# Sums of weights loaded one at a time, and the last unit's second half added on VectorE

## The chip, the cores and the metric

The kernel runs on one core of a Trainium2 chip. The metric is the device time of one execution in microseconds; lower is better. Engines are named as in the profile: PE (TensorE, matrix products), PEld (its weight loads), DVE (VectorE), ACT (ScalarE), POOL (GpSimd), and SP (SyncE, which here only issues transfers). The core has 16 DMA engines, which all queues share.

## The reference, cut to what matters

One decoder block over 512 tokens plus 16 meta tokens, width 1024. After a LayerNorm the input is projected by `w_in` (1024 x 10240) to the queries, keys, values and gates of two attention branches of 8 and 16 heads, and to two merge gates:

```python
proj = jnp.einsum('bld,dn->bln', h, w_in[i])
q_d, k_d, v_d, g_d, q_s, k_s, v_s, g_s, m_d, m_s = jnp.split(proj, IN_OFFSETS, axis=-1)
...
outs_d.append(diff_attn_block(q_d[:, :, :, t0:t1], k_d[:, :, :, :t1], v_d[:, :, :t1], q_pos, slopes, lam))
outs_s.append(stick_breaking_block(q_s[:, :, t0:t1], k_s[:, :, :t1], v_s[:, :, :t1], q_pos))
...
br_d = jnp.einsum('blw,wd->bld', y_d * jax.nn.silu(g_d), w_br_diff[i])
br_s = jnp.einsum('blw,wd->bld', y_s * jax.nn.silu(g_s), w_br_sb[i])
merged = jax.nn.sigmoid(m_d + b_gate[i, 0]) * br_d + jax.nn.sigmoid(m_s + b_gate[i, 1]) * br_s
y = jnp.einsum('bld,de->ble', merged, w_out[i])
h = layer_norm(DN_ALPHA * h + y, ln_g[i], ln_b[i])
```

All of it is float32 at the interface.

## The kernel before, in words

**Products.** A float32 factor is split into a rounded high part and the rest, and a product is three matmuls: high by high, high by low, low by high. For weights, `prep` makes the split of one tile of 128 x 512: ACT writes `wh` (L183), DVE subtracts to get `wl` (L188). `wh` and `wl` have six buffers each, and `prep` is called four tiles ahead of the product that reads the tile.

**Units.** The work between the projections is 16 units in a row: eight `d` units (a differential head each, softmax) and eight `s` units (two stick-breaking heads each). During unit u the kernel also projects the keys and values of unit u+1 and the queries of unit u+2. Keys are computed position by position into `ks` and then stored by SP into the two key tiles `k` (L646, L647), eight small transfers per unit; the scores of the next unit (L759) read them, and a store can only start once the scores of the unit before have read the old keys.

**Sums of weights.** From the sixth unit on (`SEVEN = 5`), keys and values together are made with seven products of half-size blocks in place of eight. Three of the seven weight operands of a unit are sums of blocks of `w_in`: they are held in tiles `rawk` (five buffers). SP loads the first term (L144) and POOL's own DMA queue adds the others with an accumulating transfer (L146), four of these for each of the 11 units. `fetch` issues the loads whose buffers are free, sums first, and puts each accumulate on a list `later`, due 3 or 6 calls of `prep` later; `prep` calls `fetch` once. The pool of the `rawk` tiles is opened in unit `u + 4 == SEVEN`, that is u = 1. A helper, `placed`, holds each accumulate behind the POOL instruction that the program names before it; the first stage (up to `keep_order`) is held in program order too. Transfers on SP are not held so: the tile framework's scheduler places them by what they depend on. POOL runs its instructions in order; a POOL instruction that waits holds all behind it.

**POOL's other work in this stretch.** The bias of each `d` unit (L827, two buffers, so that it waits for the unit two before), the copy of meta columns (L663), and in each `s` unit two accumulating transfers `ys` (L935): the two heads of a unit leave PSUM in the wrong halves of the partitions, so ACT copies one half to `half` (L933), crossing partitions, and the other to `y` (L934), and POOL's transfer adds `half` to `y`.

**The last unit (p = 7).** Its `y` is the tile `ysT` itself. After it, DVE multiplies the gate in (L528), and DVE and ACT prepare the operands of the branch products (`operands`, L1038 to L1045), in tiles `gh`, `gl`, `t` that reuse the memory of the attention's tiles, `half` among them.

**Sync.** Each transfer on SP or ACT takes the next of eight semaphores in turn, so that the transfer eight places on waits until this one has landed.

Of the kernel before, what the change touches and what calls it, by code (L numbers as in the profile page):

```python
# [13 lines left out]
ALU = mybir.AluOpType  # L14
# [23 lines left out]
SEVEN = 5  # L38
# [7 lines left out]
def hybrid_block_kernel(ctx: ExitStack, tc: tile.TileContext, x, meta, emb_g, emb_b, w_in, b_gate,  # L46
                        diff_lambda, subln_g, w_br_d, w_br_s, w_out, ln_g, ln_b, out):
    nc = tc.nc
    v, s, g, pe = nc.vector, nc.scalar, nc.gpsimd, nc.tensor
# [76 lines left out]
    sum_loads, other_loads = [[l for l, x in enumerate(loads) if (x[2] == "rawk") == y] for y in (True, False)]  # L126
# [6 lines left out]

    def fetch(most=99):

        for order in (sum_loads, other_loads):
            while order and most:
                l = order[0]
                src, more, tag = loads[l]
                bufs, log = rings[tag]  # L140
                if len(log) >= bufs and left[log[-bufs]] or tag not in pools:
                    break
                raw = pools[tag].tile([P, 4, P], F32, tag=tag, name=tag, bufs=bufs)
                nc.sync.dma_start(raw if l < WOUT else raw.rearrange("p a b -> p (a b)"), src)  # L144
                if more is not None:
                    second[l] = [lambda raw=raw, x=x: g.dma_start(raw, x, accum_op=ALU.add) for x in more]  # L146
                    if tag == "rawa":
                        added(l)
                    else:
                        for n in range(len(more)):  # L150
                            later.append((state["n"] + 3 + 3 * n, lambda l=l: added(l)))
                        later.sort(key=lambda x: x[0])
                raws[l] = raw
                log.append(order.pop(0))
                most -= 1

    def added(l):

        if second.get(l):
            placed(second[l].pop(0), ORDERED[3:])  # L160
# [61 lines left out]
    def placed(work, engines=ORDERED):  # L222

        ins = nc.cur_bb.bb.instructions
        n = len(ins)
        work()
        for e in engines:
            new = next((i for i in ins[n:] if i.engine == e), None)
            old = next((ins[m] for m in range(n - 1, max(n - 400, 0), -1) if ins[m].engine == e), None)
            if new is not None and old is not None:  # L230
                follow(new, old)
# [153 lines left out]
    def query(n, o, w, k):  # L385

        pe.matmul(pss[n][:, ds(o, w)], raw0[:, n, k, :], hF[k][:, ds(M + o, w)], start=(k == 0), stop=(k == KT - 1))  # L387
# [3 lines left out]
    def high(half, k, copy):  # L391

        copy(hTh[:, k, HALF[half]], hF[k][:, HALF[half]])
# [55 lines left out]
    def lam2():  # L449
# [3 lines left out]
                 y=lambda h, k: query(1, 256 * h, 256, k), s=lambda h, k: high(h, k, s.copy),  # L453
# [129 lines left out]
    with tc.tile_pool(name="att", bufs=1) as ap:  # L583
# [334 lines left out]
        def s_values(unit, c, p, ta):  # L918
            V = unit["V"]
            v4, a4 = tails[c]  # L920
            own, oth = ((LO, HI), (HI, LO))[c]
            av = pav.tile([P, 512], F32, tag="av", name="av")
            pe.matmul(av, V[c][:, 0, :], ta[0][0], start=True, stop=False)
            pe.matmul(av[:, QOFF[4]:], v4, a4, start=False, stop=False)
            for j in range(1, 4):
                o = av[:, QOFF[j]:]
                pe.matmul(o, V[c][:, j, :], ta[j][0], start=False, stop=False)  # L927
                pe.matmul(o, V[c][:, j, :], ta[j][1], start=False, stop=False)
            pe.matmul(av, V[c][:, 0, :], ta[0][1], start=False, stop=True)
            if "y" not in unit:  # L930
                unit["y"] = gpool.tile([P, S], F32, tag="sg", name="ys")
            half = ap.tile([P, S], F32, tag="sq", name="half")
            s.copy(half[own], av[oth])  # L933
            s.copy(unit["y"][own], av[own])  # L934
            placed(lambda: g.dma_start(unit["y"][own], half[own], accum_op=ALU.add), ORDERED[3:])  # L935

        def keys_values(unit, kind, n):
            if UNITS.index((kind, n)) >= SEVEN:
                return [stage_kv(unit, kind, n)]
            return [stage_k(unit, kind, n), stage_v(unit, kind, n)]  # L940

        def spread(gen, t0, dt, count):
            return [(t0 + dt * m, lambda: next(gen)) for m in range(count)]
# [11 lines left out]
        pending = []  # L955
        for u, (kind, n) in enumerate(UNITS):
            unit = units[u]
            if u + 4 == SEVEN:
                pools["rawk"] = ap
            last = u + 1 == len(UNITS)  # L960
            proj = [] if last else keys_values(units[u + 1], *UNITS[u + 1])
            if u + 2 < len(UNITS):
                proj.append(stage_q(units[u + 2], *UNITS[u + 2]))
            steps = pending + [(0.6, lambda unit=unit: values(unit, kind))]
            pending = []
            if u + 1 < SEVEN:
                steps.append((9.2, store_k))
            if u in range(SEVEN - 5, SEVEN - 1):
                if not tS:
                    tS.append(ypool.tile([P, KT, L], F32R, tag="ys", name="tS"))  # L970
                steps.append((8.0, lambda k=u + 5 - SEVEN: placed(lambda: input_sums(k))))
            if u in GATE_AT and u < 14:
                proj.append(raw_gate(GATE_AT[u], kept["r"][GATE_AT[u]]))
            if kind == "d":
                ta = {}
                dt, t0, t1 = TD[u in GATE_AT]
                steps += spread(d_scores(unit, n), 0.0, dt, 10)
                parts = transposed(ta, apads[n % 2], "d")
                steps += [(t0 + 0.7 * m, f) for m, f in enumerate(parts)]
                steps.append((t1, lambda: d_values(unit, ta)))  # L980
                pending = [(3.0 if n < 7 else 5.8, lambda unit=unit, n=n: d_norm(unit, n))]
            else:
                if n == 0:
                    diag.append(ap.tile([P, L], F32, tag="bias", name="diag", bufs=2))
                    g.memset(diag[0], 0.0)
                    g.tensor_copy(diag[0][:, L - P:], ident)
                    for a in apads:
                        for i in range(NB):
                            g.memset(a[:, ds(AOFF[i] + NKEY[i] - 1, 1)], 0.0)
                if last:  # L990
                    ydT = [pair_of("ydT", n=S) for k in range(4)]
                    ydT = [ydT[k % 4][:, k // 4, :] for k in range(8)]
                    ysT = ypool.tile([P, 8, S], F32, tag="ys", name="ysT")
                    ysT = [ysT[:, k, :] for k in range(8)]
                    unit["y"] = ysT[7]

                    def fill_in(y, of):
                        placed(lambda: nc.sync.dma_start(y, of), [mybir.EngineType.SP])

                    fill_in(ydT[7], kept["d"][7])  # L1000
                    for m, (y, of) in enumerate(((ydT, "gd"), (ysT, "gs"))):
                        for j in range(7):
                            steps.append((1.3 + 1.5 * (7 * m + j), lambda o=y[j], x=kept[of][j]: fill_in(o, x)))
                    proj += [gate("d", n, lambda: ydT[7]), merge_gate(0, 0), merge_gate(0, 1), merge_gate(0, 2),
                             gate("s", n, lambda: ysT[7])]
                else:
                    if GATE_AT.get(u) == n:
                        yd = gpool.tile([P, S], F32, tag="sg", name="yd")
                        nc.sync.dma_start(yd, kept["d"][n])
                        proj.append(gate("d", n, lambda yd=yd: yd, kept["gd"][n]))  # L1010
                    else:
                        steps += zip((12.0, 24.0), late_gate(ap, *(kept[x][n] for x in ("d", "r", "gd"))))
                    proj.append(gate("s", n, lambda unit=unit: unit["y"], kept["gs"][n]))
                for c in range(2):
                    ta = {}
                    steps += spread(s_scores(unit, c, n == 0), (2.0 + 4.3 * c) if n == 0 else 4.4 * c, 0.85, 5)
                    parts = transposed(ta, apads[c], c)
                    steps += [(7.0 + 6.5 * c + 0.7 * m, f) for m, f in enumerate(parts)]
                    steps.append((10.5 + 6.5 * c, lambda c=c, ta=ta: s_values(unit, c, n, ta)))
            run(proj, steps)  # L1020
# [235 lines left out]
```

## Time and profile before

| | |
|---|---|
| time, median of 3 runs | 729.81 us (729.35 to 733.26) |
| the profiled execution's own time | 724.71 us |
| its span (first to last instruction) | 722.9 us |
| PE busy | 706.7 us (98%) |
| DVE busy | 571.3 us (79%) |
| ACT busy | 434.1 us (60%) |
| POOL busy | 127.6 us (18%) |
| mean granted PE clock | 0.996 |

A line of the profile reads "engine line operation out<-in"; a time in brackets is how long the engine sat idle before the instruction, and the name behind the arrow is what ended that. Busy time of matmuls counts their pipelined ends, so the idle time in brackets is a little shorter than the delay from start to start.

### The profile page before, as it was taken

Reading aid. Unit: us, or ns where it says so; the run is one execution under the profiler, and the core shown is the slowest. Engines: PE = TensorE matmul, PEld = TensorE weight load, DVE = VectorE, ACT = ScalarE, POOL = GpSimd, SP = SyncE. Lnnn points to the kernel's source line nnn. Section 1 sums busy time; section 2 is a strip of 40 time slices with the busy share of each in tenths; the row PEclk is TensorE's granted clock in tenths of the full one; section 3 lists DMA queues with packets and bytes.
Section 4 is the critical chain, followed back from the end, with each engine's and each line's share of the span. In section 5 each row is a group of like instructions: output and inputs, shape, how many; then the busy total and the mean of one; then the engine's idle time right before and its main releaser. Section 6 shows DMA issues by size and latency. Waiting matters only on the chain.

```text
span 722.9 us, 13508 instructions
## 1 busy us (share of the span) xinstructions
PE 706.7 (98%) x4558; PEld 644.5 (89%) x4558; DVE 571.3 (79%) x1253; ACT 434.1 (60%) x1043; POOL 127.6 (18%) x153
## 2 busy tenths in 40 slices
PE   9998999999999999999999999999999999999994
PEld 8998999989999888989989899988878998999884
DVE  6886897887796767979887898976267888788887
ACT  5674776767576677867767586765356456555300
POOL 3251110122122120212132110000003202130002
PEclk9999999999999999999999999999999999999998
DMA  9398544778989795798897956556539837787902
GB/s 293 95 171 180 158 101 122 171 159 194 217 170 201 196 183 153 163 234 165 219 208 177 227 137 188 146 154 190 167 90 197 173 108 186 142 167 195 325 18 102
DMA packets 182343, 123.64 MB, mean 171 GB/s; under 512 B 9041, under 2 KB 165106, under 8 KB 182274
## 3 DMA queue, kind: packets, MB, share of 16 engines
q1 hardware_dynamic: 148130, 102.32, 49.0%
q0 software_dynamic: 33824, 19.40, 21.6%
q10 hardware_dynamic: 320, 1.06, 0.4%
q8 instruction: 36, 0.59, 0.3%
q14 instruction: 33, 0.27, 0.1%
HBM read 91.96 MB, written 9.44 MB: 140 GB/s over the span
## 4 chain that ended last, share of the span: by engine, by line
PE 79%; DMA 6%; DVE 6%; ACT 4%; issue 3%; POOL 1%; SPq 0%; ACTq 0%; DVEq 0%; POOLq 0%
PE q L693 15%; PE ps L496 10%; PE ps L497 10%; PE ps L498 10%; PE q L1063 8%; PE ps L512 7%; PE sc L759 5%; PE t L765 3%; DMA k<-ks 2%; PE t L770 1%; DMA lgb<-in_ln_b_dram 1%; DMA ss<-sm 1%; PE bank L387 1%; PE av L927 1%; ACT wh L183 1%
## 5 line engine op out<-in xcount | busy, mean ns | idle before, releaser
L188 DVE TENSOR_TENSOR wl<-raw,wh 128x512 fp32r<-128x512 f32 x169 | 114.8, 686 | 45.8 <-ACT wh L183 40.9
L496 PE MATMUL ps<-hTh,wh 128*128 128x512 f32 x368 | 144.6, 393 | 1.5 <-ACT wh L183 1.5
L497 PE MATMUL ps<-hTl,wh 128*128 128x512 f32 x368 | 144.7, 393 | 0.0
L498 PE MATMUL ps<-hTh,wl 128*128 128x512 f32 x368 | 144.6, 393 | 0.0
L183 ACT CAST wh<-raw 128x512 fp32r<-128x512 f32 x169 | 103.0, 620 | 35.3 <-PE ps L497 26.4
L496 PEld LDWEIGHTS ps<-hTh,wh 128*128 128x128 f32 x368 | 69.2, 188 | 15.2 <-ACT wh L183 1.9
L146 POOL DMA_DIRECT2D rawk<-in_w_in_dram x44 | 58.7, 1649 | 131.2 <-DMA rawk<-in_w_in_dram 49.5
L498 PEld LDWEIGHTS ps<-hTh,wl 128*128 128x128 f32 x368 | 69.1, 188 | 14.0 <-DVE wl L188 0.4
L497 PEld LDWEIGHTS ps<-hTl,wh 128*128 128x128 f32 x368 | 69.2, 188 | 13.1
L759 PE MATMUL sc<-k,A 128*128 128x264 f32 (+3 forms) x320 | 67.9, 300 | 3.3 <-DMA k<-ks 3.1
L1063 PE MATMUL q<-gh,wh 128*128 128x256 f32 x224 | 63.5, 283 | 0.3 <-ACT t L1072 0.3
L1063 PE MATMUL q<-gl,wh 128*128 128x256 f32 x224 | 63.4, 283 | 0.0
L1063 PE MATMUL q<-gh,wl 128*128 128x256 f32 x224 | 63.4, 283 | 0.0
L776 DVE TENSOR_TENSOR al<-t,ah 128x512 fp32r<-128x512 f32 (+2 forms) x88 | 45.6, 525 | 22.2 <-ACT ah L775 18.4
L913 DVE TENSOR_TENSOR_SCAN e<-e,diag 128x528 f32<-128x528 f32 (+1 forms) x64 | 53.8, 846 | 7.0 <-ACT e L907 7.0
L775 ACT CAST ah<-t 128x288 fp32r<-128x288 f32 (+3 forms) x88 | 39.9, 462 | 29.9 <-PE t L765 20.0
L759 PEld LDWEIGHTS sc<-k,A 128*128 128x128 f32 x320 | 50.5, 189 | 6.5 <-issue 3.4
L693 PE MATMUL q<-tS,wh 128*128 128x264 f32 x176 | 50.8, 290 | 0.0
L693 PE MATMUL q<-tl,wh 128*128 128x264 f32 x176 | 50.3, 286 | 0.0
L693 PE MATMUL q<-tS,wl 128*128 128x264 f32 x176 | 50.0, 285 | 0.0
L512 PE MATMUL ps<-hTh,wh 128*128 128x264 f32 x160 | 46.1, 288 | 0.0
L512 PE MATMUL ps<-hTh,wl 128*128 128x264 f32 x160 | 45.8, 287 | 0.0
(291 smaller groups left out, 1843.4 us busy)
## 6 DMA issues: line engine op xcount, KB each, us to landing
raw<-in_w_in_dram SPq DMA_DIRECT2D x141, 256.0 KB, 3.4
rawk<-in_w_in_dram POOLq DMA_DIRECT2D x44, 256.0 KB, 6.0
rawk<-in_w_in_dram SPq DMA_DIRECT2D x33, 256.0 KB, 4.1
k<-ks SPq DMA_DIRECT2D x60, 132.0 KB, 3.6
raw<-in_w_out_dram SPq DMA_DIRECT2D x16, 256.0 KB, 3.2
k<-ks SPq DMA_DIRECT2D x60, 66.0 KB, 3.4
A<-low SPq DMA_DIRECT2D x28, 128.0 KB, 3.3
raw<-in_w_br_diff_dram SPq DMA_DIRECT2D x12, 256.0 KB, 3.9
```

The source lines that it names most:

```text
L146: second[l] = [lambda raw=raw, x=x: g.dma_start(raw, x, accum_op=ALU.add) for x in more]
L183: s.copy(wh, raw)
L188: eng.tensor_tensor(wl, raw, wh.bitcast(F32), op=ALU.subtract)
L496: pe.matmul(ps, wh[:, k % 4, :], hTh[:, k, M:], start=(k == 0), stop=False)
L497: pe.matmul(ps, wh[:, k % 4, :], hTl[:, k, M:], start=False, stop=False)
L498: pe.matmul(ps, wl[:, k % 4, :], hTh[:, k, M:], start=False, stop=(k == KT - 1))
L512: pe.matmul(ps[:, :H2], a[:, k % 4, :], b[:, k, ts(c, H2)], start=(k == 0 and m == 0), stop=(k == KT - 1 and m == 2))
L693: pe.matmul(bank, a[:, k, :], b, start=start and k == 0 and j == 0, stop=k == 3 and j == 2, skip_group_check=not start)
L759: pe.matmul(ps[:, :n], q, K[:, m, k0:k0 + n], start=(m == 0), stop=(m == 1))
L776: v.tensor_tensor(l, t[:, o:o + w], h.bitcast(F32), op=ALU.subtract)
L913: v.tensor_tensor_scan(rev, rev, diag[0][:, L - nk:][:, ::-1], 0.0, ALU.mult, ALU.max)
L1063: pe.matmul(bank, a[:, k, :], b[:, n, k, :], start=start and k == 0 and m == 0, stop=k == 3 and m == 2, skip_group_check=not start)
```

## The change

It has two parts. `fetch` issues at most one load of a sum at each call, and the pool of the sums opens one unit later (`u + 3`, that is u = 2). And in the last unit DVE adds the PSUM half to `half` directly into `ysT`, in place of ACT's second copy and POOL's accumulating transfer.

```diff
     def fetch(most=99):
-        for order in (sum_loads, other_loads):
+        for order, most in ((sum_loads, 1), (other_loads, most)):
             while order and most:
...
             half = ap.tile([P, S], F32, tag="sq", name="half")
             s.copy(half[own], av[oth])
+            if p == 7:
+                v.tensor_tensor(unit["y"][own], av[own], half[own], op=ALU.add)
+                return
             s.copy(unit["y"][own], av[own])
             placed(lambda: g.dma_start(unit["y"][own], half[own], accum_op=ALU.add), ORDERED[3:])
...
-            if u + 4 == SEVEN:
+            if u + 3 == SEVEN:
                 pools["rawk"] = ap
```

The order of the instructions on each engine shows where it acts. SP's queue reads the same in both programs, 366 rows: the loads of the first five `rawk` tiles stay where they were, ahead of seven loads of `raw`. What moves is POOL's queue.

POOL in units 0 to 3, before (L663 copies the meta columns, L827 makes a bias, L146 adds a term to a sum):

```order
L663 COPY hF<-hM 128x2x16
L827 TENSOR_SCALAR bias<-bias 128x528
L146 DMA rawk<-in_w_in_dram 128x4x128 x5
L663 COPY hF<-hM 128x2x16
L146 DMA rawk<-in_w_in_dram 128x4x128 x2
L827 TENSOR_SCALAR bias<-bias 128x528
L663 COPY hF<-hM 128x2x16
L827 TENSOR_SCALAR bias<-bias 128x528
L663 COPY hF<-hM 128x2x16
L827 TENSOR_SCALAR bias<-bias 128x528
L146 DMA rawk<-in_w_in_dram 128x4x128
```

POOL at the same place, now:

```order
L663 COPY hF<-hM 128x2x16
L827 TENSOR_SCALAR bias<-bias 128x528
L663 COPY hF<-hM 128x2x16
L827 TENSOR_SCALAR bias<-bias 128x528
L146 DMA rawk<-in_w_in_dram 128x4x128
L663 COPY hF<-hM 128x2x16
L146 DMA rawk<-in_w_in_dram 128x4x128 x3
L827 TENSOR_SCALAR bias<-bias 128x528
L146 DMA rawk<-in_w_in_dram 128x4x128 x2
L663 COPY hF<-hM 128x2x16
L146 DMA rawk<-in_w_in_dram 128x4x128
L827 TENSOR_SCALAR bias<-bias 128x528
```

The first seven accumulates leave their place behind the second bias: four now stand behind the third, three behind the fourth. From the eighth on the two orders agree until the `s` units.

POOL in the `s` units, before (L935 adds the `half` of a unit):

```order
L146 DMA rawk<-in_w_in_dram 128x4x128 x2
L935 DMA ys<-half 64x512 x2
L146 DMA rawk<-in_w_in_dram 128x4x128 x4
L935 DMA ys<-half 64x512 x2
L146 DMA rawk<-in_w_in_dram 128x4x128 x4
L935 DMA ys<-half 64x512 x2
```

POOL there now (L938 is the L935 of before):

```order
L146 DMA rawk<-in_w_in_dram 128x4x128
L938 DMA ys<-half 64x512
L146 DMA rawk<-in_w_in_dram 128x4x128
L938 DMA ys<-half 64x512
L146 DMA rawk<-in_w_in_dram 128x4x128 x3
L938 DMA ys<-half 64x512
L146 DMA rawk<-in_w_in_dram 128x4x128
L938 DMA ys<-half 64x512
L146 DMA rawk<-in_w_in_dram 128x4x128 x3
```

One accumulate of each unit's four, the last, now stands behind the next unit's first `ys` in place of ahead of it; this happens five times.

DVE in the last unit, now (the two L935 are new; the other rows stand as before, and ACT has lost its two L934 and POOL its two L935 for `ysT`):

```order
L935 TENSOR_TENSOR ysT<-av,half 64x512
L776 TENSOR_TENSOR al_6886<-t_6879,ah_6885 128x416
L188 TENSOR_TENSOR wl<-raw,wh 128x512
L526 TENSOR_TENSOR sg<-ps,sg 128x512
L796 TENSOR_TENSOR a_448<-t_6879,a_448 16x32
L776 TENSOR_TENSOR al_6904<-t_6897,ah_6903 128x288
L776 TENSOR_TENSOR al_6908<-t_6897,ah_6907 128x160
L935 TENSOR_TENSOR ysT<-av,half 64x512
L528 TENSOR_TENSOR ysT<-sg,ysT 128x512
```

The second L935 now stands directly ahead of the gate product L528.

## The prediction

> **What bounds the kernel now.** I read the page's busy shares first, then the waits of PE, then a table of PE by stages, and only then the neighbourhood of each wait. The busy share:
>
> ```profile
> PE 706.7 (98%) x4558; PEld 644.5 (89%) x4558; DVE 571.3 (79%) x1253; ACT 434.1 (60%) x1043; POOL 127.6 (18%) x153
> ```
>
> PE is the bound. Only what PE itself waits for can be won, and there is little of that. The waits of PE, longest in total first, and PE's busy time by stages:
>
> ```profile
> PE sc L759 <- DMA k<-ks: 3.1, 2, 2.2
> PE ps L496 <- ACT wh L183: 1.5, 1, 1.5
> ...
> 75.00:300.00 225.00, 224.81 (x1497) 207.42 (x1496) 178.43 (x477) 154.68 (x392) 36.65 (x37) 1.00 0.73 169
> ...
> 325.00:525.00 200.00, 200.00 (x1242) 179.39 (x1242) 156.09 (x294) 129.59 (x328) 27.00 (x25) 1.00 0.73 179
> ...
> 550.00:700.00 150.00, 149.65 (x976) 137.27 (x975) 122.22 (x222) 71.35 (x136) 22.73 (x20) 1.00 0.69 169
> ```
>
> In the three long stages PE (the first figure behind the length) is never idle for more than 0.35 us in sum, so what is won ahead of them is carried through them. Between them lie three waits, on the timeline of PE (start, length, and in brackets the idle time and what ended it):
>
> ```profile
> 59.78 0.29 PE L512 MATMUL ps<-hTl,wh 128*128 128x264 f32 x1
> 59.91 0.28 PE L512 MATMUL ps<-hTh,wl 128*128 128x264 f32 x1
> 62.43 0.49 PE L759 MATMUL sc<-k,A 128*128 128x264 f32 x2 [2.23 <-DMA k<-ks]
> ...
> 317.70 0.23 PE L927 MATMUL av<-ah,V 128*128 128x160 f32 x1
> 318.81 0.36 PE L759 MATMUL sc<-k,A 128*128 128x264 f32 x1 [0.88 <-DMA k<-ks]
> ...
> 531.27 0.39 PE L497 MATMUL ps<-hTl,wh 128*128 128x512 f32 x1
> 531.49 0.39 PE L498 MATMUL ps<-hTh,wl 128*128 128x512 f32 x1
> 533.40 0.50 PE L496 MATMUL ps<-hTh,wh 128*128 128x512 f32 x1 [1.52 <-ACT wh L183]
> ...
> 534.46 0.40 PE L496 MATMUL ps<-hTh,wh 128*128 128x512 f32 x1
> ```
>
> Counted from start to start, the first costs 62.43 - (59.91 + 0.13) = 2.39 us, since the row before it shows the pace of 0.13. The second costs 318.81 - (317.70 + 0.08) = 1.03, with 0.08 for the narrow matmul, an estimate by its width from the same pace. At the third, the matmul at 534.46 is the fourth after the one at 531.49; at the pace of 0.23 it was due at 532.41, so the loss is 2.05. Together 5.47 us; the question is how much of each the change removes.
>
> **The change, part by part: the seven early accumulates.** POOL's timeline, and the DMA view of 38 to 64 us (q0 is POOL's queue, q1 SP's; issues with KB each and the median us to landing), with the key stores of the next stretch, 64 to 90 us, below:
>
> ```profile
> 38.49 6.78 POOL L146 DMA_DIRECT2D rawk<-in_w_in_dram  x5
> ...
> 56.48 1.28 POOL L146 DMA_DIRECT2D rawk<-in_w_in_dram  x1 [7.49 <-DMA rawk<-in_w_in_dram]
> 57.26 2.54 POOL L827 TENSOR_SCALAR bias<-bias 128x528 f32<-128x528 f32 x1
> 58.74 1.21 POOL L663 COPY hF<-hM 128x32 f32<-128x32 f32 x1
> ...
> q0 software_dynamic: 3696, 1.84, 55.8%
> q1 hardware_dynamic: 6119, 3.40, 54.5%
> ...
> k<-ks SPq DMA_DIRECT2D x4, 132.0 KB, 5.0
> k<-ks SPq DMA_DIRECT2D x4, 66.0 KB, 7.7
> ...
> k<-ks SPq DMA_DIRECT2D x4, 132.0 KB, 2.4
> ```
>
> The two queues together fill the engines in these 26 us, and POOL's seven accumulates are half of it: 0.558 x 26 / 7 = 2.07 us of all 16 engines each. A key store of 132 KB takes 5.0 us there, and 2.4 where POOL's queue is empty. The store that held PE, from the chain of waits:
>
> ```profile
> 56.89 5.40 DMA k<-ks
> ...
> 312.74 5.94 DMA k<-ks
> ```
>
> Now the accumulates stand behind the third bias, which starts at 57.26 and waits for DVE, not for them. What stood behind that bias started at 58.74, so the first accumulate is issued at about 58.7, and the stores of before run without any. With 2.4 us the store issued at 56.89 lands at 59.3, ahead of 60.04, when PE wants it. With the landing time halfway between 2.4 and 5.0 it lands at 60.6 and PE still waits 0.5 us. The bounds of this term are 0 and 2.39 us; nothing in it can cost PE time at this place, because the accumulates leave. I take 2.39, as the row without POOL's queue is the nearest to the new state.
>
> The moved accumulates are not needed soon, by the tile `rawk` alone: its transfers' issues on POOL and casts on ACT (shortest, median and longest in ns, first and last start), and the time to landing:
>
> ```profile
> L146 POOL DMA_DIRECT2D rawk<-in_w_in_dram x44: 1273/1299/3499, 38.5 to 429.9; - x44
> L183 ACT CAST wh<-rawk x44: 602/621/681, 120.7 to 449.1; 128x512 fp32r<-128x512 f32 x44
> ...
> DMA to landing us min/median/max: 2.9/5.4/14.4
> ```
>
> Three of them are issued behind the fourth bias, at about 83 us; with the longest landing of any transfer into a sum, 14.4 us, they are there before 100, and the first cast is at 120.7. The cover is 20 us. POOL's bias and column copies move by issues of 1.3 us and are used a unit later. SP's queue keeps its order, so nothing is queued anew behind a waiting transfer.
>
> **The five late accumulates.** The fourth accumulate of a unit now waits behind the next unit's first `ys`. POOL's timeline there, and the cast of that sum on ACT:
>
> ```profile
> 311.95 1.28 POOL L146 DMA_DIRECT2D rawk<-in_w_in_dram  x1 [7.14 <-DMA rawk<-in_w_in_dram]
> 321.04 0.85 POOL L935 DMA_DIRECT2D ys<-half  x1 [7.80 <-ACT ys L934]
> ...
> 339.27 0.62 ACT L183 CAST wh<-rawk 128x512 fp32r<-128x512 f32 x1
> ```
>
> The accumulate at 311.95 ran beside the key store of 312.74, the one that made PE wait at 318.81. It goes to 321.9. That frees up to 2.07 us of the engines ahead of the store's landing at 318.68, and 1.03 less is enough. The bounds are 0 (the store is held by SP's own transfers) and 1.03; I take 0.8, since the larger part of the traffic there stays. The sum then has 339.3 - 321.9 = 17.4 us to land, longer than the longest 14.4. The same holds, unit by unit, for the other four.
>
> **The last unit.** The chain of waits from 525 to 534 us, with ACT's copy and a DVE product from PSUM of the same length ahead of it:
>
> ```profile
> 514.74 0.68 DVE L526 TENSOR_TENSOR sg<-ps,sg 128x512 f32<-128x512 f32 x1
> ...
> 524.01 0.58 ACT L933 COPY half<-av 64x512 f32<-64x512 f32 x1 [5.07 <-PE av L929]
> 528.82 0.41 ACT L1044 CAST gh<-ydT 128x256 fp32r<-128x256 f32 x1 [3.62 <-DMA ysT<-half]
> ...
> 525.49 3.15 DMA ysT<-half
> ...
> 528.76 0.09 DVE ysT L528
> ...
> 532.84 0.52 ACT wh L183
> ```
>
> The transfer is on the path twice: DVE's gate product L528 needs its sum, and ACT's first `gh` reuses the memory of `half` and may only start when it has been read. From 528.76 on it is ACT and DVE alone that lead to the cast `wh` of 532.84, for which PE waits. Now `half` ends at 524.59 and DVE adds: between 0.58 (ACT's copy) and 0.69 for one pass over 512 columns, I take 0.68 from the row. The gate product then starts at about 525.35 in place of 528.76, 3.4 us earlier, and `wh` is ready at 533.36 - 3.4 = 530.0, ahead of 531.72, when PE wants it. All 2.05 us go, with 1.7 to spare; bounds 1 and 2.05. The two new adds, 1.36 us on DVE, replace 1.16 on ACT; the first falls at about 512.7, between two subtractions of which the second waits for ACT anyway.
>
> **The sum.** 2.39 + 0.8 + 2.05 = 5.24 us. Against the profiled execution that is 724.71 - 5.2 = 719.5, its span 717.7. The runs shown have a median of 729.81, 5.1 above the profiled one; I carry the same gain over, 724.6. A difference under 0.5% (3.65 us) can hardly be told from no change in this kernel.
>
> **The rivals.** First, that one of the larger waits stays, because SP's own queue, with nearly as much traffic, holds the key store: then 5.24 - 2.39 = 2.85 are won, 727.0. Against it speaks the 2.4 us of the next stretch. That the first edit does little is part of this: the words speak of loads, and SP's loads have not moved at all; only POOL's accumulates have.
>
> Second, the jam moves on with the accumulates. Of the stores for unit 2 the last for the first head is issued at 81.35, and PE reads at 86.97:
>
> ```profile
> 81.35 0.61 SPq L647 DMA_DIRECT2D k<-ks  x1
> ...
> 86.97 0.65 PE L759 MATMUL sc<-k,A 128*128 128x264 f32 x4
> ```
>
> Two accumulates are issued at about 83. If the store then took 7.7 us, as those of 66 KB did in the jam of 38 to 64 us, PE would wait 81.35 + 7.7 - 86.97 = 2.1: 726.7. Against it: two accumulates are 4.1 us of the engines, and they start when the store has run for most of its 2 us.
>
> Third, slower than before: the five late sums come too late. The place is the cast at 339.27 and its four like. It decides from a landing of 17.4 us on; each microsecond above costs PE up to one, five times, and the gain is used up at 18.5. At 19.5 us the time is 724.6 + 10.5 = 735.1. For it speaks only that POOL now issues in a busier place; against it the longest landing of 14.4. [...] The longest issue of an accumulate in this trace took 3.5 us, 2.2 above the median, which would leave the cover standing and the time as it is.
>
> **How the numbers follow.** All three waits gone, or nearly: 0.64, 724.6 (own range 723.4 to 726). One of the larger stays: 0.16, 727.0. The jam moves: 0.11, 726.7. Late sums: 0.05, above 730. That leaves 0.04 for what none of these names. The range takes in the second and third case with the spread of the runs, and reaches below the full 5.47 (724.3) by 1.7 us, about a third as much again, since the runs are longer than the profiled one and may hold more of the same waits: 722.6 to 727.9. Faster: the first case and a third of the second and third, 0.72. Slower: 0.06. The rest, 0.22, within 0.5%.
>
> **What would show it.** In the changed profile the rows "PE sc L759 <- DMA k<-ks" and "PE ps L496 <- ACT wh L183" are gone from PE's waits; PE's busy share rises, its busy time stays near 706. POOL's first accumulate starts after 57 us, and the key store of about 56 us lands within 3 us. The gate product of `ysT` follows the last copy of `half` within 1.5 us. The prediction is wrong if PE shows a new wait, for a key store near 85 us or for a cast of a sum in the `s` units, or if the waits go and the span does not follow.

## The result and the profile after

The changed kernel takes 719.46 us (median of 4 runs: 719.61, 719.31, 718.85, 722.77), the kernel before 729.58 in the same comparison (729.35, 733.26, 729.81, 724.82): a ratio of 0.9886, 95% interval 0.9849 to 0.9922. The forecast was 724.6 with a range of 722.6 to 727.9; the change brought more. A longer comparison on one chip (below) gives 719.87 against 726.39, ratio 0.9905 (0.9884 to 0.9926). The profiled execution has 719.61 us and a span of 717.8, where 719.5 and 717.7 had been worked out. So the steps came out for the profiled execution, and the base they were carried to did not; that the span agrees to 0.1 us is partly luck, since a second trace of the changed kernel (below) has 717.4. Two later executions of the kernel before, of 1805 and 4007 us, stand far from all others and are left out of the counts and spreads below.

The busy share on the page:

```profile
PE 705.1 (98%) x4558; PEld 643.9 (90%) x4558; DVE 572.1 (80%) x1255; ACT 433.2 (60%) x1041; POOL 126.4 (18%) x151
```

PE's waits, longest in total first (us in total, times, longest):

```profile
PE warm L308 <- POOL idents masks.py:199: 1.4, 1, 1.4
...
PE q L1066 <- ACT t L1075: 0.2, 1, 0.2
```

The waits for `k` and for `wh` are gone; what is left is the start of the program (two rows for `bank`, 0.9 us in sum, are among it) and rows of 0.2 us. PE by stages, with the two short stretches that held the second and third wait (length, then PE's busy time):

```profile
300.00:325.00 25.00, 25.00 (x167) 22.89 (x167) 21.63 (x41) 16.89 (x44) 4.53 (x4) 1.00 0.96 208
...
525.00:550.00 25.00, 25.00 (x112) 20.68 (x112) 20.44 (x36) 15.87 (x28) 5.24 (x4) 1.00 0.79 170
```

PE is busy from end to end in both. The first wait's place, on the timelines of PE, POOL and SP's queue:

```profile
59.87 0.28 PE L512 MATMUL ps<-hTh,wl 128*128 128x264 f32 x1
59.99 0.40 PE L759 MATMUL sc<-k,A 128*128 128x264 f32 x2
...
58.66 1.52 POOL L146 DMA_DIRECT2D rawk<-in_w_in_dram  x1
...
50.58 1.33 SPq L646 DMA_DIRECT2D k<-ks  x2
...
54.12 0.62 SPq L646 DMA_DIRECT2D k<-ks  x1
```

the median landing of these stores from 38 to 64 us,

```profile
k<-ks SPq DMA_DIRECT2D x4, 132.0 KB, 2.8
```

and SP's queue at the same place before:

```profile
50.61 3.14 SPq L646 DMA_DIRECT2D k<-ks  x2
...
56.89 0.62 SPq L646 DMA_DIRECT2D k<-ks  x1
```

PE's read of `k` follows at the pace of 0.12 us. The first accumulate starts at 58.66. The key stores land sooner (a median of 2.8 us, 5.0 before). The one that held PE is also issued 2.8 us earlier, at 54.12 in place of 56.89, behind an issue that took 1.33 us and not 3.14. But the late issue belongs to the first trace of before alone. In the four other traces that have this wait (two of before among them, further down) it is issued at 54.2 to 55.0 and still lands only at 61.6 to 62.4, after 6.6 to 7.6 us. From the chain of waits in the second and in the third trace of before:

```profile
54.23 7.57 DMA k<-ks
...
54.74 7.32 DMA k<-ks
```

So the landing is what held PE, as the prediction had it. The last unit, on DVE and ACT:

```profile
521.13 0.69 DVE L935 TENSOR_TENSOR ysT<-av,half 64x512 f32<-64x512 f32 x1 [5.32 <-ACT half L933]
521.86 0.69 DVE L528 TENSOR_TENSOR ysT<-sg,ysT 128x512 f32<-128x512 f32 x1
...
520.51 0.58 ACT L933 COPY half<-av 64x512 f32<-64x512 f32 x1 [5.07 <-PE av L929]
```

DVE's add takes 0.69 us, and the gate product starts 1.35 us after ACT's last copy of `half` does (4.75 us before: 528.76 after 524.01). The sums are not late: among the transfers into `rawk` the longest landing is now 10.8 us in place of 14.4.

### The profile page after: what moved, and what is told of

Read it like the earlier page. It is cut to its first block, busy times and chain, and to the rows that moved or that the text cites. A ratio compares the mean times of both kernels' runs of the same rounds, so it can differ in the third digit from the quotient of the medians.

```text
span 717.8 us, 13500 instructions
## 1 busy us (share of the span) xinstructions
PE 705.1 (98%) x4558; PEld 643.9 (90%) x4558; DVE 572.1 (80%) x1255; ACT 433.2 (60%) x1041; POOL 126.4 (18%) x151
## 4 chain that ended last, share of the span: by engine, by line
PE 86%; DVE 5%; DMA 3%; ACT 3%; issue 1%; POOL 1%; SPq 0%; ACTq 0%; DVEq 0%; POOLq 0%
PE q L693 15%; PE ps L496 12%; PE ps L497 12%; PE ps L498 12%; PE q L1066 10%; PE ps L512 7%; PE sc L759 6%; PE t L765 4%; PE t L770 1%; DMA lgb<-in_ln_b_dram 1%; PE av L927 1%; PE bank L387 1%; PE tv L726 1%; PE av L928 1%; DVE hr L1216 1%
## 5 line engine op out<-in xcount | busy, mean ns | idle before, releaser
L146 POOL DMA_DIRECT2D rawk<-in_w_in_dram x44 | 60.9, 1669 | 95.8 <-DMA rawk<-in_w_in_dram 40.8
L938 POOL DMA_DIRECT2D ys<-half x14 | 11.8, 840 | 197.0 <-ACT ys L937 187.2
```

## The experiments

The first theory after the result, called stretch theory: something makes waits for transfers longer in the runs than in the profiled execution, and the change takes them away with their spread. The rival, called constant theory: the spread belongs to the execution, and the change is worth a constant 5.2 us. Four kernels on one chip, with 28 runs of before shared between them. The first is the kernel before itself, for a second trace; no edit.

> The kernel before, once more, under the same rounds. Constant theory (the three waits are worth 5.2 us in every execution, and the spread of 724.8 to 733.3 us belongs to the execution, not to the kernel): a spread of several us like the one seen, and the changed kernel beside it spreads as much, 5.2 us lower at equal rank. Stretch theory (the waits for transfers are longer in the runs than in the profiled execution, and the change removes them together with their spread): most runs at 728 to 733, the lowest near 724.8, while the changed kernel stays within 2 us of 719.4. Against the kernel before itself the ratio is 1.000 within 0.003.

Measured: 726.09, ratio 0.9993 (0.9969 to 1.0018), range 723.9 to 731.9; the 728 to 733 that stretch theory had for most runs did not come. Its profiled execution happened to be the longest, 731.93 us with a span of 730.2, 7.2 above that of the first trace. PE's waits in it:

```profile
PE sc L759 <- DMA k<-ks: 3.9, 2, 2.1
PE q L1063 <- ACT t L1068: 2.5, 1, 2.5
PE ps L496 <- ACT wh L183: 1.5, 1, 1.5
...
PE q L1063 <- ACT t L1072: 0.7, 1, 0.7
```

There is a fourth wait at 668 us, which the first trace showed with 0.3 us, and the middle one is twice as long. All delays of PE, from start to start, are 11.1 us against 7.4; that is half of the 7.2. Most of the other half stands in the clock. Four intervals of 3.41 us around the first wait in this trace (PE's busy time and matmuls first, the granted clock third from the end of a row):

```profile
55.77:59.17 3.40, 3.40 (x17) 2.78 (x16) 2.83 (x9) 1.03 (x3) 2.94 (x3) 1.00 1.22 236
59.18:62.59 3.41, 1.35 (x10) 1.12 (x9) 0.73 (x3) 1.12 (x2) 0.53 (x2) 1.00 1.29 224
62.60:66.00 3.40, 3.40 (x18) 3.40 (x17) 1.01 (x5) 0.91 (x3) 0.00 (x0) 0.50 1.18 280
66.02:69.40 3.38, 3.38 (x30) 3.38 (x29) 2.57 (x8) 1.62 (x5) 0.00 (x0) 1.00 0.20 45
```

and in the first trace of before:

```profile
58.14:61.55 3.41, 2.06 (x11) 1.56 (x9) 1.92 (x6) 1.12 (x2) 1.82 (x2) 1.00 1.26 240
61.56:64.96 3.40, 2.53 (x21) 2.56 (x22) 1.04 (x5) 0.48 (x1) 0.00 (x0) 1.00 1.08 298
```

Behind the wait PE ran 3.41 us at half clock (below, a half-clock stretch), 18 matmuls where 30 go at the full one; the same again behind the middle wait, from 322.0. In the first trace the same wait was longer (2.23 us idle against 2.06) and had no such stretch.

Second, the first part of the change alone: the hunks of `fetch` and `u + 3`.

```diff
+            if p == 7:
+                v.tensor_tensor(unit["y"][own], av[own], half[own], op=ALU.add)
+                return
```

is left out.

> The first part of the change alone (one load of a sum at a call, the pool opened a unit later); the last unit keeps its transfer. Constant theory: 3.2 us off at equal rank (2.39 and 0.8), profiled span about 719.7. Stretch theory, if the key stores are what stretches: 8 us off the median and a spread of 2 us. If it is the last unit's transfer that stretches: 3.2 us off and the spread stays.

Measured: 724.36, ratio 0.9971 (0.9953 to 0.999). Third, that hunk alone:

> The second part alone (DVE's add in the last unit); the accumulates stay where they were. Constant theory: 2.05 us off at equal rank, profiled span about 720.9. Stretch theory, if the last unit's transfer stretches: 6 to 7 us off the median. If the key stores stretch: 2 us off and the spread stays at 4 to 8 us.

Measured: 722.93, ratio 0.9951 (0.9928 to 0.9974). Fourth, the changed kernel:

> The changed kernel once more, on the same chip as the two parts. Constant theory: the sum of the two parts, 5.2 us below the kernel before at equal rank and as wide a spread. Stretch theory: 9 to 10 us below its median, most runs within 1 us of 719.4.

Measured: 719.87, ratio 0.9905 (0.9884 to 0.9926), range 719.2 to 721.2. The two parts alone gain 2.0 and 3.5 us, together 6.5. Neither theory had the sizes: constant theory had 5.2 in every execution, with as wide a spread, and stretch theory 9 to 10. The spread of before in this comparison, 723.4 to 732.1, shrinks to 2 us with the change (one of the four earlier runs of the changed kernel, 722.77, lies outside; it has no trace). PE's waits in the trace of the first part alone,

```profile
PE ps L496 <- ACT wh L183: 1.5, 1, 1.5
...
PE q L1063 <- ACT t L1068: 0.9, 1, 0.9
PE q L1063 <- ACT t L1072: 0.7, 1, 0.7
```

and in that of the second:

```profile
PE q L1066 <- ACT t L1071: 2.8, 1, 2.8
PE sc L759 <- DMA k<-ks: 2.0, 1, 2.0
```

Each part removes its own waits (the middle one happens to be missing from the second trace too, although nothing there removes it). The fourth wait is in both, and the second part's trace has a half-clock stretch behind each of its two.

What makes the clock fall was tried next: the changed kernel with sixteen waits of PE put in by hand, two in each pair of branch products.

```diff
+        def held(q):
+            n = 1 + state["held"] % 8
+            state["held"] += 1
+            wh = split[h + q][1]
+            for _ in range(n):
+                s.copy(wh, wh.bitcast(F32))
...
         s.copy(u, x)
+        held(1)
...
         s.copy(w, x)
+        held(3)
```

> The changed kernel with sixteen waits of PE put in by hand, two in each of the eight pairs of branch products: behind ACT's copy of a product's bank, ACT casts the next product's weights once more in place, one to eight times, so that PE waits by some 0.6 us a cast more each time. No result changes. Plain theory: a wait costs its length and nothing else; the granted clock stays whole through all sixteen, and the span grows by the sum of the waits. Half-clock theory: behind waits of some 2 us and more stands a stretch of 3.4 us at half clock, now and then for the short ones, nearly always for those above 4 us, and none behind those under 1.5 us; the span then grows by the sum of the waits and 1.7 us more for each such stretch, about 10 stretches, 17 us.

The span is 796.1, 78.3 above the changed kernel's. The sixteen delays sum up to 55.3 of that from start to start. Waits of 0.98, 1.04 and twice 1.63 us had no half clock behind them; the twelve from 2.28 to 5.54 us all had, in twelve stretches of one or two times 3.41 us, where about 10 with a cost of 17 us were expected. PE had work in 52.8 us of them; at the pace measured in the next experiment that costs 22.6 us, close to the other 23. A short wait and a longer one (the interval of the wait, then the next):

```profile
554.64:558.03 3.39, 1.76 (x15) 1.56 (x14) 1.05 (x2) 2.82 (x6) 1.28 (x1) 1.00 1.18 233
558.06:561.40 3.34, 3.34 (x30) 3.34 (x29) 2.81 (x7) 0.86 (x3) 0.00 (x0) 1.00 0.52 66
564.88:568.27 3.39, 1.37 (x11) 1.37 (x12) 0.87 (x2) 2.43 (x5) 1.82 (x2) 1.00 0.27 80
568.29:571.69 3.40, 3.02 (x15) 2.73 (x13) 1.10 (x2) 1.23 (x4) 0.75 (x1) 0.50 1.12 180
```

The starts of all stretches lie on one grid: 568.28, 575.11, 585.35, ..., 732.12 are whole multiples of 3.413 us apart. That gave a sharper theory, tried with sixteen equal waits (`n = 3` in place of the first line of `held`):

> The changed kernel with sixteen waits of PE as in the earlier run with holds, all of them now by three casts of ACT: 2.3 us idle each. No result changes. Grid theory: the half-clock stretches start on one grid of 3.413 us, and one follows a wait where more than half of an interval of that grid, 1.7 us, was idle; 2.3 us fit into one interval with more than 1.7 in two cases of three, so 10 or 11 of the 16 waits have a stretch behind them, and which ones follows from the grid that the stretches themselves show. Length theory: a wait of over 2 us always has one, 16 of 16. Each stretch costs 1.75 us, so the span tells the two apart as well: 16 x 2.4 + 11 x 1.75 = 57.6 or 16 x 2.4 + 16 x 1.75 = 66.4 above the changed kernel's.

Twelve of the sixteen had a stretch, and the span is 775.1, 57.3 above the changed kernel's: 57.6 had been worked out for the grid, 66.4 for the length. That the span agrees so closely is partly luck, since one or two stretches more came than were expected and each cost less; the count of twelve is what tells the theories apart. One wait that the grid cuts in two, and the next, which lies in one interval:

```profile
601.83:605.23 3.40, 2.19 (x19) 1.98 (x17) 1.93 (x4) 1.14 (x3) 0.00 (x0) 1.00 0.04 11
605.25:608.64 3.39, 2.35 (x19) 2.35 (x20) 1.29 (x2) 2.10 (x5) 0.00 (x0) 1.00 0.00 2
608.66:612.05 3.39, 1.11 (x10) 0.91 (x9) 0.69 (x1) 2.78 (x6) 0.00 (x0) 1.00 0.53 153
612.08:615.47 3.39, 3.39 (x19) 3.39 (x18) 1.72 (x3) 1.23 (x3) 0.00 (x0) 0.50 0.27 77
```

The first wait left 1.2 us idle in one interval and 1.0 in the next, and the clock stayed; the second left 2.28 in one, and it fell. The four without a stretch had at most 1.77 us in one interval, the twelve with one at least 2.1. The pace of PE inside and behind such a stretch:

```profile
562.96 0.41 PE L1066 MATMUL q<-gl,wh 128*128 128x256 f32 x1
563.17 0.41 PE L1066 MATMUL q<-gh,wl 128*128 128x256 f32 x1
...
565.22 0.28 PE L1066 MATMUL q<-gh,wh 128*128 128x256 f32 x1
565.34 0.28 PE L1066 MATMUL q<-gl,wh 128*128 128x256 f32 x1
```

0.21 us from start to start against 0.12: a stretch in which PE has work costs 3.41 x (1 - 0.12 / 0.21) = 1.5 us, a little less than the 1.7 that was taken. The span agrees: 57.3 less the sixteen delays of 2.44 leaves 18.2 for twelve stretches.

Which of the two edits of the first part does what? The opening alone (`u + 3`, `fetch` as before):

```diff
-            if u + 4 == SEVEN:
+            if u + 3 == SEVEN:
```

> The kernel before with only the later opening of the ring for the sums, and without the limit of one load with each split: the early accumulates leave the place of the first wait, the late ones stay in their old order, and the last unit stays. If the opening is what removes the first wait, the key store of about 55 us lands within 3 us, PE waits there no more, and the wait near 319 us (1.0 us in one trace of before, 2.0 in another, none in a third) and the one at 533 us stay: 2.4 us less than before in a trace, 2 to 4 in the median of the runs. If the limit is needed for it, the first wait stays at 2 us or more and the time is that of before.

Measured: 724.47, ratio 0.9958 (0.9936 to 0.998), 2.2 below its before, with the middle and the last wait in the trace and none at 60 us, as the first expectation said. (The trace itself is only 0.35 us below the first one of before, since the fourth wait takes 2.0 us in it.) And the limit alone:

```diff
-        for order in (sum_loads, other_loads):
+        for order, most in ((sum_loads, 1), (other_loads, most)):
```

> The kernel before with only the limit of one load with each split: the late accumulates of a unit stand behind the next unit's first addition of values, and of the seven early ones four still stand ahead of the third bias. If the limit is what removes the middle wait, PE has none near 319 us, while the first wait is 1 us or more, since four accumulates are still issued in its place, and the one at 533 us stays: 0 to 2 us less than before in a trace and in the median. If spreading the loads alone clears the jam, both of the first two waits go and the time is that of the first two edits together, 724.4 where before is 726.4.

Measured: 722.07, ratio 0.9932 (0.9905 to 0.9958). PE's waits with the opening alone,

```profile
PE ps L496 <- ACT wh L183: 1.5, 1, 1.5
...
PE sc L759 <- DMA k<-ks: 0.9, 1, 0.9
```

and with the limit alone:

```profile
PE q L1063 <- ACT t L1068: 2.8, 1, 2.8
PE ps L496 <- ACT wh L183: 1.5, 1, 1.5
```

With the limit alone both waits for `k` go, although four accumulates are still issued at 38 to 44 us. Its rows for 38 to 64 us (before: q1 54.5%, q0 55.8%, and 5.0 us):

```profile
q1 hardware_dynamic: 6815, 3.81, 61.6%
q0 software_dynamic: 2869, 1.43, 44.3%
...
k<-ks SPq DMA_DIRECT2D x4, 132.0 KB, 4.1
```

The engines are nearly as full as before (61.6 and 44.3%, together 105.9, against 110.3), so the jam is not cleared but eased: the next accumulate after the four starts only at 58.21, and the stores land soon enough for PE. This is the second of the two expectations, though its time, that of both edits, is missed by 2.3 us. The opening by itself takes only the first wait. The limit with the opening (724.36) was not faster than the limit alone; their intervals just overlap, so which is faster isn't decided. The fourth wait, treated next, was in both traces, 2.0 and 3.0 us long.

That wait stands behind ACT's casts of the merged sums, which wait for POOL's accumulates; ACT in the second trace of before:

```profile
659.10 0.62 ACT L1104 CAST mh<-ss 128x512 fp32r<-128x512 f32 x1 [6.24 <-DMA ss<-td]
...
661.81 0.62 ACT L1104 CAST mh<-ss 128x512 fp32r<-128x512 f32 x1 [1.57 <-DMA ss<-sm]
...
667.56 0.37 ACT L1068 COPY t<-q 128x256 f32<-128x256 f32 x1
```

So the cast was issued later, in three kernels: the changed one, before, and the first part.

```diff
-        wait = 6 if j < 6 else 1
+        wait = 8 if j < 6 else 1
```

> The changed kernel, where the cast of a merged sum on ACT is issued eight products behind its accumulate in place of six. The fourth wait, for ACT's copy of a bank at about 660 us, was 0.35 us in both traces of the changed kernel, 0.5 to 2.7 in those of before. If ACT stands there behind a cast that waits for an accumulate, the row of PE's waits for t goes and the time is 0.4 us below the changed kernel's in most runs, with no run of it 2 us above its median: 719.5 where before is 726.4. If the wait has another cause, it stays at 0.35 us and the time is the changed kernel's, 719.9.

Measured: 719.62, ratio 0.9897 (0.9867 to 0.9927). The row of waits for `t` is gone, another of 0.3 us has come (PE `pso` L1191 for ACT's `wo0h`), and the time cannot tell 719.5 from 719.9. One run, 721.88, is more than 2 us above the median, against the expectation. It is no faster version.

> The kernel before, with nothing of the change, where the cast of a merged sum on ACT is issued eight products behind its accumulate in place of six. If the fourth wait, at 660 to 672 us, is part of what the runs of before hold above the profiled one, it goes: 1.5 to 3 us less than before in the median, with the three waits of the change still in the trace. If the runs are longer for a reason outside the waits, the time is before's less the 0.5 us of its first trace, 726.

Measured: 725.69, ratio 0.9997 (0.9979 to 1.0015). The wait is gone there too, but the median does not move: a miss of the theory that the fourth wait lifts it. In the third trace of before (below) it is 0.4 us.

> The first two edits (limit and opening), without the last unit's, and the later cast of the merged sums. What is left of waits is the last unit's alone, 1.7 us from start to start with 1.5 us idle, too short for a half-clock stretch: 719.6 + 1.7 = 721.3 with a spread as small as that of the changed kernel. If the two kernels with the first two edits alone and with all were apart by more than their waits, the time is 722.5 or above.

Measured: 721.93, range 721.2 to 723.3, ratio 0.9943 (0.9923 to 0.9962), where 721.3 was expected. The ratio is 0.28% below that of the first part with the old cast, about the 2.0 us that its trace showed, though the two intervals overlap.

Last, the kernel before for a third trace:

> The kernel before once more, for a third trace of it. Wait theory: PE's time from its first to its last matmul, less its waits and less 1.7 us for each half-clock stretch, is 705 to 706.5 us again, as in the nine traces so far, however long the execution; at the fourth wait PE stands 0.5 to 3.5 us. Base theory: a longer execution has a longer remainder, by 2 us or more.

Measured: 723.82 us, span 722.0, no wait at 319 us, 0.4 at the fourth (just under the 0.5 expected), no half-clock stretch:

```profile
PE sc L759 <- DMA k<-ks: 2.2, 1, 2.2
PE ps L496 <- ACT wh L183: 1.5, 1, 1.5
```

With all traces the wait theory can be reckoned up: the end of the last matmul, less PE's delays from start to start (those above 0.25 us), less 1.5 us for each half-clock stretch.

| trace | span | delays | stretches | remainder |
|---|---|---|---|---|
| before, first | 722.9 | 7.4 | 0 | 706.3 |
| before, second | 730.2 | 11.1 | 2 | 706.5 |
| before, third | 722.0 | 6.3 | 0 | 706.0 |
| before, later cast | 726.2 | 6.8 | 2 | 706.6 |
| opening alone | 722.6 | 6.7 | 0 | 706.1 |
| limit alone | 722.9 | 6.4 | 1 | 705.7 |
| first part | 720.9 | 4.9 | 0 | 706.5 |
| first part, later cast | 719.4 | 3.4 | 0 | 706.5 |
| second part | 725.9 | 7.6 | 2 | 706.1 |
| changed | 717.8 | 2.5 | 0 | 705.5 |
| changed, again | 717.4 | 1.9 | 0 | 706.0 |
| changed, later cast | 719.6 | 2.0 | 0 | 705.7 |

Spans from 717 to 730 leave the same remainder within 1.1 us. In the last row, whose span is some 2 us longer than those of the changed kernel, the rest is a tail of 11.8 us behind the last matmul in place of 9.9.

The mean granted clock of each run says the same without a trace, roughly, since the tail counts in it too (granted 0.50 from 716.9 us to the end at 722.9 in the first trace of before). One stretch lowers it by 0.5 x 3.41 / 726 = 0.0023. Of 76 runs of before, 37 have a clock of 0.995 or more and a median of 725.4; 32 have 0.993 or 0.994 and 727.3; 7 have less, and 730.3.

## Why the prediction was wrong

**The failed step** is in the sum: "The runs shown have a median of 729.81, 5.1 above the profiled one; I carry the same gain over". The waits were priced in the one execution and the base taken from three others, as if the 5.1 us between them were a constant that the change leaves alone. They are not: the changed kernel has no such distance between its profiled execution (719.61) and its median (719.46). Two parts of it can be told apart. First, a median of 76 runs of before is 726.3, of which the profiled 724.71 lies near the low end; these 1.6 us are, by the table above, waits and half-clock stretches that the first trace happened to have short or not at all. Its own first wait, 2.23 us idle, lay 1.35 on one side of the grid and 0.88 on the other. Of the four traces of before, the one with the later cast among them, two have two stretches and two have none, one on the mean, 1.5 us; the waits removed take their stretches with them. So the change is worth 5.2 + 1.5 = 6.7 by the traces, an estimate, and 6.5 measured (726.39 to 719.87). Second, the three runs shown were 3 us above that median; 7 of the 76 later ones are as high as the lowest of the three. Three such runs out of three would be rare by chance alone, under one in a thousand by that count, and what those executions held isn't shown: there is no trace of one of them. The second trace of before, at 731.93, shows that waits and stretches can reach such a time; that they did so there is argued from the changed kernel, which in the same comparison (719.46) ran as it did later (719.87).

**The first edit and the first wait**: 2.39 of 2.39 us, as taken, and by the mechanism named: the stores land sooner (a median of 2.8 us, 5.0 before). The late issue of the store in the profiled execution was not needed for the wait, since the four other traces have the wait without it. The price that was missing is the stretch behind the wait, in three of the five traces that have this wait.

**The middle wait**: 0.8 taken, 1.03 gained in the profiled execution. Its size varies: 1.0, 2.0, none and 1.4 us in the four traces of before. None of the eight traces with the limit has it, and four of the six without, the opening's among them, do. In those four the store that PE waits for takes 5.9 to 7.3 us to land; with the limit the median of these stores is 3.5 to 4.7. That it was the accumulate at 311.95 is not shown separately from the four other moves of its kind.

**The last unit**: 2.05 taken. The wait is gone and the product follows in 1.35 us, under the 1.5 that was named; alone it gains 3.5 us in the median, more than its wait (1.7 us between neighbouring rows, 2.05 by the longer count of the prediction). One of eight traces with this wait had a stretch behind it (the one of before with the later cast), so that is 0.2 us on the mean; the rest, 1.2 us or more, is not explained. It may be noise: the 95% interval of that gain, 1.9 to 5.2 us, takes in 2.05 + 0.2.

**The rivals** did not come. PE's reads of `k` for unit 2 wait for nothing, no larger wait stayed, and no sum is late. The longest issue of an accumulate took 2.9 us, 1.5 above the median, where it was 2.2 above in the trace of before. Busy time stayed (705.1).

**The range** reached 1.7 us below the full gain "since the runs are longer than the profiled one and may hold more of the same waits". That was the right reason, and it should have been the forecast: on the profiled execution's base the sum gives 719.5. (The 0.72 for faster adds up to 0.73.)

**What stays open**: why the fourth wait, 0.4 to 3.6 us in traces of before and 2 to 3 in those with one part, was 0.4 in both traces of the changed kernel; what the excess of the second part alone is, if it is one; and what the three runs near 730 us held.

## What to carry to other kernels

Price a change against the execution in which its waits were read, and when the runs of a kernel spread over more than a per cent, ask first whether the spread is itself made of the waits that go. A wait of the matmul engine cost its length here and, where it left 1.8 us or more of one interval of the clock's grid idle, some 1.5 us more, so the same wait was cheap in one execution (the first one of before, 2.23 us idle, no stretch) and dear in the next (2.06 us idle, a stretch). At full clock, waits under 1.4 us were free of that price, so by these numbers cutting a 2 us wait to 1.4 can save up to 1.5 us more than the difference, an estimate.

## What the runs showed of the hardware

The half-clock stretches of one trace begin on one grid of 3.413 us. In the first kernel with waits put in by hand the starts listed above lie 2, 5 and 48 steps of 163.84 / 48 = 3.4133 us behind the first of them, within 0.01 us; the two of the second trace of before, at 62.60 and 322.00, lie 76 steps apart. The grid's place against the program differs from execution to execution. Counted from the first instruction, its points lie 1.15 us past whole multiples of the step in that trace, 1.67 and 1.08 in the two kernels with waits put in by hand (568.28; 560.87), and 0.11 in the first trace of before, where it is taken from the fall of the clock in the tail, at 716.91. At full clock, all 30 intervals in which PE was idle for 1.8 us or more were followed by an interval at half clock (24 of them in the two kernels with waits put in by hand); of those with 1.4 to 1.8 us one of eight was, and below 1.4 none. The one of the eight was behind the `wh` wait with 1.52 us, in the kernel before with the later cast:

```profile
532.85:536.24 3.39, 1.87 (x7) 1.13 (x7) 2.89 (x5) 3.37 (x7) 0.00 (x0) 1.00 0.00 0
536.27:539.60 3.33, 3.33 (x9) 2.58 (x8) 3.09 (x8) 1.82 (x4) 0.00 (x0) 0.50 0.84 241
```

Why that one and not the others of 1.5 to 1.77 isn't known. A wait of 2.06 us, with all of it in one interval, was enough for a stretch in the second trace of before.
